# First FFN column pair by eight plain block products, with the token sums on VectorE and used from the second pair on

## The chip, the cores and the metric

The kernel runs on one core of a Trainium2 chip. A core has a matrix engine (TensorE, in the profile PE), three engines for elementwise work (VectorE or DVE, ScalarE or ACT, GpSimd or POOL), and a queue (SyncE or SP) that issues DMAs between the chip's memory and the core's on-chip buffers. Each engine takes its instructions in a fixed order and waits for others through semaphores. TensorE writes to eight banks of 128 x 512 float32 (PSUM), from which ScalarE and VectorE copy results out. The metric is the device time of one execution in microseconds (us).

## What is computed

The reference is one layer of a sequence encoder over 1024 tokens of width 1024: three token mixers (two kinds of attention and a state-space scan) merged through gates, then a gated MLP with a causal depthwise convolution. The change touches the MLP's first matrix product alone:

```python
def conv_ffn(h, w_up, conv_w, conv_b, w_down):
    a = causal_dwconv(h @ w_up, conv_w, conv_b)        # 3 taps, along the tokens
    gate, val = jnp.split(a, 2, axis=-1)               # 2 x 2816 columns
    return (jax.nn.silu(gate) * val) @ w_down

x = x + merged @ w_out[l]
x = x + conv_ffn(rms_norm(x, norm_ffn_g[l]), ...)
```

## The kernel before

**Stages.** The mixers take most of the time. Then follow, without a break on TensorE, the output product (`wo`, lines 1326 to 1391) with the second norm, the FFN's up products (lines 1394 to 1525) and its down products (`dn`, line 1628 the matmul). Every float32 product is made of three matmuls on a high and a low part of each operand: high x high, high x low, low x high. `split` (lines 142 and 143) makes the parts: ScalarE rounds to the high part, VectorE subtracts it to get the low part.

**Pairs.** The up product has 2 x 22 blocks of 128 columns. Pair i is gate block i and value block i + 22. A product (`product`, line 1321) is 12 matmuls: one 128-column block, four blocks of 128 input rows, 512 tokens, three part combinations. With the tokens in two halves and the input rows in two halves, the normed input is four blocks: B11 and B21 (first 512 tokens, input rows 0 to 511 and 512 to 1023), B12 and B22 (last 512 tokens). Computed directly, a pair is eight products, two for each of gate and value in each half of the tokens.

**Seven products.** The kernel uses a Strassen-Winograd scheme with seven products for each pair. On the side of the weights it needs S12 (two sums and differences of gate and value blocks) and S34 (two more), made by `sums` on GpSimd (lines 1411 to 1415) and then split into wh and wl; h22 is the split lower half of the value block. On the side of the tokens it needs T1 = B12 - B11, T3 = B22 - B12, T2 = T3 + B11 and T4 = B21 - T2. T1 takes the place of B12 in the norm itself (`norm2`); T3 is kept there in float32 as `T3f`. Once, at the first pair, `t_split` splits T3f into cbh and cbl (four blocks each, lines 1444 and 1447), `t_sums(True)` turns T3f into T2 in place (1454, 1455), which is split, and `t_sums(False)` turns it into T4 (1457, 1458), which is split. In `t_sums` blocks 0 and 1 are summed on VectorE, 2 and 3 on GpSimd. A pair's products are, by bank: `ua` gate x B11, then gate x B21 into the same bank; `ub` S12 x T2; `uc` S12 x T1, then S34 x B22; `ud` S34 x T3, then h22 x T4. A second product into a bank starts after ScalarE has copied out the first (to cg at 1431 or 1473, e5 at 1491, e7 at 1496). VectorE and GpSimd combine the copies to cg (gate) and cv (value), the convolution runs as ScalarE and VectorE steps (`fa`, 1517 and 1520), then SiLU (1523), a multiplication (1524) and a store to `act_d`.

**Early gate products.** Of the first four pairs (FIRST = 4) the two `ua` products, which need no T2, T3 or T4, are made ahead: B11 products of 0, 1 and 2, the last tile's norm, their B21 products, then both products of 3. So the loop has five products for each of pairs 0 to 3 and seven from pair 4 on.

**Order and buffers.** TensorE's order is that of the code; the other engines' order is set by a scheduler when the kernel is built. Raw weight blocks of a pair (tag wr) have two buffers, one for the gate and one for the value block; the gate block's is free when S34 has been made, the value block's when h22 has been split. S12, S34 and h22 have one buffer each; wh and wl have three in turn. Gate blocks 1 to 3 are loaded ahead into other buffers (tag t4).

## Time and profile before

| | us |
|---|---|
| median of 3 runs | 2163.03 |
| lowest and highest run | 2156.59, 2163.8 |
| the profiled execution | 2163.26 |
| its span in the profile | 2161.5 |

The profile covers one execution. Its views used below are the page's first lines (busy time of each engine), the chain of waits that ended last, busy time by stretch, and the timeline, whose rows are: start in us, duration in us, engine, line, operation, output<-inputs, and in brackets the idle time before the instruction with what ended it. DVE, ACT and POOL starts are some 0.1 us earlier than the end of the instruction before, so that the cost of one in a row of several is read between starts.

### The profile page before, as it was taken

To read this page: it belongs to the slowest core of one execution; us is meant where nothing else is said; L and a number is where in the kernel's file an instruction comes from. 1 tells how busy PE (TensorE), PEld (TensorE's weight loads), DVE (VectorE), ACT (ScalarE), POOL (GpSimd) and SP (SyncE) were. 2 spreads that over 40 slices of the span, in tenths; PEclk is the share of its full clock that TensorE was granted. 3 is DMA by queue.
4 is the path that set the end of the run, shared out by engine and by line. 5 is a ranking of instruction groups with operands and counts; after the bars stand their busy time and mean duration, and the time that the engine had idled before them with its cause. 6 is when DMAs were issued, how large, how long until landed. Compare 5 with 4: busy or idle time off the path is not lost.

```text
span 2161.5 us, 29107 instructions
## 1 busy us (share of the span) xinstructions
PE 2053.6 (95%) x10239; PEld 1693.8 (78%) x10253; DVE 1406.9 (65%) x2574; ACT 933.7 (43%) x1669; POOL 689.9 (32%) x636
## 2 busy tenths in 40 slices
PE   7999899999999999999999999999889999999999
PEld 6898787778888787787666788888668888887887
DVE  6687477356656566665888446557976777665655
ACT  5554222145555555554445313223444444544432
POOL 2454132212222222220222022002655454441855
PEclk9999999999999999999999999999899999999999
DMA  5167668554343544524343556342122222229765
GB/s 168 33 186 223 228 211 247 196 147 126 100 131 108 125 125 107 128 87 119 92 117 94 169 178 209 116 151 79 39 88 88 78 88 78 87 71 346 250 210 194
DMA packets 276649, 303.61 MB, mean 140 GB/s; under 512 B 19308, under 2 KB 209784, under 8 KB 276504
## 3 DMA queue, kind: packets, MB, share of 16 engines
q1 hardware_dynamic: 276504, 301.76, 45.5%
q8 instruction: 81, 1.33, 0.3%
q14 instruction: 64, 0.52, 0.1%
HBM read 209.03 MB, written 92.67 MB: 140 GB/s over the span
## 4 chain that ended last, share of the span: by engine, by line
PE 76%; DVE 10%; DMA 5%; ACT 3%; issue 3%; POOL 2%; SPq 0%; DVEq 0%; ACTq 0%; POOLq 0%
PE mm L794 15%; PE dn L1628 10%; PE ybr L167 8%; PE ua L1321 5%; PE uc L1321 4%; PE ud L1321 4%; PE wo L1366 4%; PE fx L167 4%; PE s L884 4%; PE tp L952 3%; PE ub L1321 2%; PE cq L167 1%; PE fxv L167 1%; PE q L167 1%; PE kv L167 1%
## 5 line engine op out<-in xcount | busy, mean ns | idle before, releaser
L794 PE MATMUL mm<-hnh,wh 128*128 128x512 f32 x576 | 251.5, 437 | 0.0
L906 POOL TENSOR_SCALAR pm<-pm,rs 128x128 f32<-128x128 f32 (+7 forms) x128 | 109.6, 859 | 407.3 <-DVE rs L905 256.2
L794 PE MATMUL mm<-hnh,wl 128*128 128x512 f32 x576 | 228.1, 396 | 0.0
L794 PE MATMUL mm<-hnl,wh 128*128 128x512 f32 x576 | 227.3, 395 | 0.0
L1628 PE MATMUL dn<-dr,dr 128*128 128x512 f32 x592 | 182.2, 389 | 0.0
L899 ACT ACTIVATE pm<-s,nmx 128x128 f32<-128x128 f32 (+2 forms) x192 | 110.0, 578 | 98.7 <-DVE nmx L896 69.8
L958 DVE TENSOR_TENSOR ptl<-tp,pth 128x512 fp32r<-128x512 f32 (+1 forms) x160 | 100.3, 633 | 69.7 <-ACT pth L957 68.0
L889 DVE TENSOR_REDUCE nmx<-s 128x1 f32<-128x128 f32 (+2 forms) x192 | 105.6, 553 | 58.8 <-PE s L887 47.0
L884 PE MATMUL s<-qk,qk 96*128 96x384 f32 (+5 forms) x480 | 122.3, 359 | 12.7 <-ACT pm L899 11.0
L957 ACT ACTIVATE pth<-tp 128x512 fp32r<-128x512 f32 (+1 forms) x160 | 88.0, 553 | 100.7 <-PE tp L952 100.2
L1628 PEld LDWEIGHTS dn<-dr,dr 128*128 128x128 f32 x592 | 111.1, 188 | 23.1
L794 PEld LDWEIGHTS mm<-hnh,wl 128*128 128x128 f32 x576 | 109.1, 189 | 25.6
L794 PEld LDWEIGHTS mm<-hnl,wh 128*128 128x128 f32 x576 | 110.2, 191 | 17.8 <-issue 3.4
L794 PEld LDWEIGHTS mm<-hnh,wh 128*128 128x128 f32 x576 | 110.7, 192 | 17.1 <-issue 3.3
L1628 PE MATMUL dn<-dr 128*128 128x512 f32 x296 | 115.2, 389 | 0.0
L167 PE MATMUL fx<-w5h,hnh 128*128 128x512 f32 x256 | 101.9, 403 | 7.0 <-ACT w5h L142 7.0
L143 DVE TENSOR_TENSOR dr<-dr,dr 128x1024 fp32r<-128x1024 f32 x52 | 73.0, 1403 | 54.3 <-ACT dr L142 52.4
L142 ACT ACTIVATE wh<-wr 128x1024 fp32r<-128x1024 f32 (+1 forms) x46 | 41.9, 911 | 144.5 <-PE ybr L167 63.5
L884 PEld LDWEIGHTS s<-qk,qk 96*128 96x128 f32 (+1 forms) x480 | 82.2, 194 | 25.6 <-ACT pm L899 15.0
L167 PE MATMUL fx<-w5h,hnl 128*128 128x512 f32 x256 | 101.8, 399 | 0.0
L167 PE MATMUL ybr<-ah,wh 128*128 128x512 f32 x256 | 99.6, 394 | 1.6 <-ACT ah L142 1.6
L167 PE MATMUL fx<-w5l,hnh 128*128 128x512 f32 x256 | 101.1, 396 | 0.0
(457 smaller groups left out, 5819.1 us busy)
## 6 DMA issues: line engine op xcount, KB each, us to landing
dr<-act_d SPq DMA_DIRECT2D x99, 256.0 KB
wr<-in_ffn_w_up_dram SPq DMA_DIRECT2D x47, 512.0 KB
wr<-in_w_in_dram SPq DMA_DIRECT2D x36, 512.0 KB
g_d<-t SPq DMA_DIRECT2D x24, 512.0 KB
gl<-g_d SPq DMA_DIRECT2D x24, 512.0 KB
ws<-in_ffn_w_down_dram SPq DMA_DIRECT2D x22, 512.0 KB
wsum_d<-ws SPq DMA_DIRECT2D x22, 512.0 KB
act_d<-fa SPq DMA_DIRECT2D x22, 512.0 KB
```

The lines of the kernel that those rows point to most:

```text
L143: return i, le.tensor_sub(l, src, f32(h))
L167: T.matmul(ps, a(k), b(k), start=(i == 0), stop=(i == n - 1))
L794: T.matmul(ps, a[:, k, :], b[half][:, k, :], start=(k == 0 and i == 0), stop=(k == NK - 1 and i == 2))
L884: T.matmul(ps[:, :w], q_[:, qs], k_[:, a:a + w], start=i_ == 0, stop=not last and i_ == len(o.passes) - 1)
L889: later(c + 0.1, lambda ps=ps, ci=ci, a=a, b=b: V.reduce_max(nmx[:, ci:ci + 1], ps[:, :b - a], axis=AX, negate=True))
L899: pss[ci][1][0] = later(c + 0.9 + 0.1 * ci, lambda ci=ci, a=a, b=b: A.activation(p_[:, a:b], pss[ci][0][:, :b - a], AF.Exp, bias=nb, accum ...
L906: G.tensor_scalar(p_[:, 0:n * P], p_[:, 0:n * P], rs[:, 3:4], 0.0, op0=ALU.mult, op1=ALU.add)
L957: later(c + 0.05, lambda th=th, pt=pt, off=off: A.activation(th[:, :off], pt[:, :off], AF.Copy))
L958: pl[0] = later(c + 0.6, lambda th=th, tl=tl, pt=pt, off=off: V.tensor_sub(tl[:, :off], pt[:, :off], f32(th[:, :off])))
L1321: T.matmul(ps, a, b, start=first and n == 0, stop=n == 11, skip_group_check=not first)
L1366: T.matmul(p, a, b, start=k == 0 and i == 0, stop=k == NK - 1 and i == 2)
L1628: T.matmul(ps[m], a[:, ts_], b[:, 512:], start=first_ and j == 0 and q == 0, stop=j == NFH - 1 and q == 2, skip_group_check=not first_)
```

## The change

Pair 0 is computed directly: its eight products are gate and value block against B11, B21, T1 and B22. With T1 in the place of B12, the products of the last 512 tokens get the first half's B11 product added, on VectorE (lines 1499 and 1500 of the changed kernel). S12, S34 and h22 aren't made for pair 0; the whole value block is split instead (hB). The early gate products go in the order 1, 2, 0 (`FORDER`), and those of block 3 follow pair 0's. All of `t_sums` is on VectorE. T3 is split at pair 0 as before, T2 after that; T4 is made and split within pair 1, where T2, T3 and T4 are used first. Pair 0's convolution (`finish_pair`) runs within pair 1.

```diff
@@ -1354,7 +1354,8 @@
     xrp = po_.enter_context(TP("x2p", 1))
     gff = bcast(norm_ffn_g[0], D, "gff", xrp)
     x2r = [None] * NT
-    first = []
+    first = {}
+    FORDER = (1, 2, 0, 3)
     units = [(t, nh) for nh in range(2) for t in range(3)] + [(t, nh) for t in range(3, NT) for nh in range(2)]
 
     head = [psp.tile([P, 512], F32, name=uid("wo"), tag="up", bufs=6) for _ in range(3)]
@@ -1370,14 +1371,14 @@
     for t, nh in units:
         ns = slice(512 * nh, 512 * nh + 512)
         if nh == 0 and 4 <= t < 4 + FIRST:
-            n = t - 4
+            n = FORDER[t - 4]
             if n == 0:
                 r0 = raws(pairs[0])
                 raw = r0[0]
             else:
                 raw = fpl.tile([P, NK, P], F32, name=uid("wr"), tag="t4", bufs=4)
                 SY.dma_start(raw, upv[:, :, pairs[n] * P:pairs[n] * P + P])
-            first.append(halves(raw) if n < 3 else raw)
+            first[n] = halves(raw) if n < 3 else raw
         if nh == 0:
             x2r[t] = xrp.tile([P, D], F32, name=uid("x2"), tag="x2", bufs=4)
             SY.dma_start(x2r[t], x[0, t * P:(t + 1) * P, :])
@@ -1396,10 +1397,14 @@
 
     B11, B21 = [(rows(h2h[0], k), rows(h2l[0], k)) for k in (0, 4)]
     T1, B22 = [(rows(h2h[1], k), rows(h2l[1], k)) for k in (0, 4)]
-    a_ = []
-    for n in range(3):
-        a_.append(bank("ua"))
+    a_, done_ = {}, {}
+
+    def p1(n):
+        a_[n] = bank("ua")
         product(a_[n], first[n], 0, *B11)
+
+    for n in FORDER[:3]:
+        p1(n)
     norm2(NT - 1, x2r[NT - 1])
     po_.close()
 
@@ -1415,22 +1420,20 @@
         G.tensor_sub(S34[:, 4:8, :], ri[:, 4:8, :], S12[:, 4:8, :])
         return S12, S34
 
-    S_ = sums(*r0)
-    h22_ = halves(r0[1][:, 4:8, :], 4)
-    done_ = []
-    for n in range(3):
-        c_ = upb.tile([P, S], F32, name=uid("cg"), tag="cg", bufs=FIRST)
-        A.activation(c_[:, 512:], a_[n], AF.Copy)
-        done_.append(c_)
-    for n in range(FIRST):
-        if n == 3:
-            first[n] = halves(first[n])
-            a_.append(bank("ua"))
-            product(a_[n], first[n], 0, *B11)
-            done_.append(upb.tile([P, S], F32, name=uid("cg"), tag="cg", bufs=FIRST))
-            A.activation(done_[n][:, 512:], a_[n], AF.Copy)
+    def keep_p1(n):
+        done_[n] = upb.tile([P, S], F32, name=uid("cg"), tag="cg", bufs=FIRST)
+        A.activation(done_[n][:, 512:], a_[n], AF.Copy)
+
+    def p2(n):
         product(a_[n], first[n], 4, *B21, first=False)
         A.activation(done_[n][:, 0:512], a_[n], AF.Copy)
+
+    for n in FORDER[:3]:
+        keep_p1(n)
+    p2(1)
+    hB = halves(r0[1])
+    p2(2)
+    p2(0)
     cbp = pcb.enter_context(TP("cb", 1))
     cbh = cbp.tile([P, 12, 512], F32R, name="cbh", tag="cbh")
     cbl = cbp.tile([P, 12, 512], F32R, name="cbl", tag="cbl")
@@ -1449,20 +1452,57 @@
     def t_sums(second):
 
         for k in range(4):
-            e = G if k > 1 else V
             if second:
-                e.tensor_add(tf[k], tf[k], f32(B11[0][k]))
-                e.tensor_add(tf[k], tf[k], f32(B11[1][k]))
+                V.tensor_add(tf[k], tf[k], f32(B11[0][k]))
+                V.tensor_add(tf[k], tf[k], f32(B11[1][k]))
             else:
-                e.tensor_sub(tf[k], f32(B21[0][k]), tf[k])
-                e.tensor_add(tf[k], tf[k], f32(B21[1][k]))
+                V.tensor_sub(tf[k], f32(B21[0][k]), tf[k])
+                V.tensor_add(tf[k], tf[k], f32(B21[1][k]))
 
     def tmp(name, bufs=1):
         return upa.tile([P, 512], F32, name=uid(name), tag=name, bufs=bufs)
 
-    for n, i in enumerate(pairs):
+    def finish_pair(i, cg, cv):
+        av = []
+        for j, c in ((i, cg), (i + NFF, cv)):
+            a = fpl.tile([P, S], F32, name=uid("fa"), tag="t4", bufs=4)
+            A.activation(a, c, AF.Identity, bias=pc_f2[:, 44 + j:45 + j], scale=pc_f2[:, j:j + 1])
+            for d in (1, 2):
+                w = pc_f1[:, 44 * (2 - d) + j:44 * (2 - d) + j + 1]
+                V.scalar_tensor_tensor(out=a[:, d:], in0=c[:, :S - d], scalar=w, in1=a[:, d:],
+                                       op0=ALU.mult, op1=ALU.add)
+            av.append(a)
+        A.activation(av[0], av[0], AF.Silu)
+        V.tensor_mul(av[1], av[0], av[1])
+        SY.dma_start(act_d[i], av[1])
+
+    t_split(T3)
+    b0 = bank("ub")
+    product(b0, hB, 0, *B11)
+    f1 = tmp("e5")
+    A.activation(f1, b0, AF.Copy)
+    product(b0, hB, 4, *B21, first=False)
+    cv = fpl.tile([P, S], F32, name=uid("cv"), tag="t4", bufs=4)
+    A.activation(cv[:, 0:512], b0, AF.Copy)
+    t_sums(True)
+    c0_ = bank("uc")
+    product(c0_, first[0], 0, *T1)
+    product(c0_, first[0], 4, *B22, first=False)
+    t_split(T2)
+    first[3] = halves(first[3])
+    d0 = bank("ud")
+    product(d0, hB, 0, *T1)
+    product(d0, hB, 4, *B22, first=False)
+    p1(3)
+    keep_p1(3)
+    p2(3)
+    V.tensor_add(done_[0][:, 512:], c0_, done_[0][:, 512:])
+    V.tensor_add(cv[:, 512:], d0, f1)
+    plain = (pairs[0], done_[0], cv)
+
+    for n, i in list(enumerate(pairs))[1:]:
         early = n < FIRST
-        ri, rj = r0 if n == 0 else raws(i)
+        ri, rj = raws(i)
         if early:
             cg = done_[n]
         else:
@@ -1472,11 +1512,14 @@
             product(a0, hA, 0, *B11)
             A.activation(cg[:, 512:], a0, AF.Copy)
         e1 = cg[:, 512:]
-        S12, S34 = S_ if n == 0 else sums(ri, rj)
+        S12, S34 = sums(ri, rj)
         hS12 = halves(S12)
         hS34 = halves(S34)
-        h22 = h22_ if n == 0 else halves(rj[:, 4:8, :], 4)
-        if n > 0:
+        h22 = halves(rj[:, 4:8, :], 4)
+        if n == 1:
+            t_sums(False)
+            t_split(T4)
+        else:
             b0 = bank("ub")
             product(b0, hS12, 4, *T2)
         if not early:
@@ -1484,20 +1527,14 @@
         c0_ = bank("uc")
         product(c0_, hS12, 0, *T1)
         d0 = bank("ud")
-        if n == 0:
-            t_split(T3)
         product(d0, hS34, 0, *T3)
         e5 = tmp("e5")
         A.activation(e5, c0_, AF.Copy)
-        if n == 0:
-            t_sums(True)
-            t_split(T2)
         e7 = tmp("e7")
         A.activation(e7, d0, AF.Copy)
         product(c0_, hS34, 4, *B22, first=False)
-        if n == 0:
-            t_sums(False)
-            t_split(T4)
+        if n == 1:
+            finish_pair(*plain)
             b0 = bank("ub")
             product(b0, hS12, 4, *T2)
         X = tmp("X", 2)
@@ -1511,20 +1548,7 @@
         G.tensor_add(cv[:, 512:], X, Y)
         V.tensor_add(cg[:, 512:], c0_, X)
         V.tensor_add(cv[:, 0:512], d0, X)
-        av = []
-        for j, c in ((i, cg), (i + NFF, cv)):
-            a = fpl.tile([P, S], F32, name=uid("fa"), tag="t4", bufs=4)
-            A.activation(a, c, AF.Identity, bias=pc_f2[:, 44 + j:45 + j], scale=pc_f2[:, j:j + 1])
-            for d in (1, 2):
-                w = pc_f1[:, 44 * (2 - d) + j:44 * (2 - d) + j + 1]
-                V.scalar_tensor_tensor(out=a[:, d:], in0=c[:, :S - d], scalar=w, in1=a[:, d:],
-                                       op0=ALU.mult, op1=ALU.add)
-            av.append(a)
-        A.activation(av[0], av[0], AF.Silu)
-        V.tensor_mul(av[1], av[0], av[1])
-        SY.dma_start(act_d[i], av[1])
-
-
+        finish_pair(i, cg, cv)
 
 
     wd = ffn_w_down[0].rearrange("(r p) c -> r p c", p=P)
```

Three places show how the instructions now stand. First GpSimd, from the last tile's norm on. S_4621 and S_4622 are S12 and S34 of pair 0, S_4648 and S_4649 those of pair 1; before:

```order
L1411 TENSOR_TENSOR S_4621_15530<-wr_15047 128x512
L1414 TENSOR_TENSOR S_4622_15533<-wr_15045,wr_15047 128x512
L1412 TENSOR_TENSOR S_4621_15530<-S_4621_15530,wr_15045 128x512
L1415 TENSOR_TENSOR S_4622_15533<-wr_15045,S_4621_15530 128x512
L1411 TENSOR_TENSOR S_4648_15763<-wr_15761 128x512
L1412 TENSOR_TENSOR S_4648_15763<-S_4648_15763,wr_15759 128x512
L1454 TENSOR_TENSOR T3f<-T3f,hnh_13413 128x512 x2
L1455 TENSOR_TENSOR T3f<-T3f,hnl_13415 128x512 x2
L1414 TENSOR_TENSOR S_4649_15766<-wr_15759,wr_15761 128x512
L1415 TENSOR_TENSOR S_4649_15766<-wr_15759,S_4648_15763 128x512
L1510 TENSOR_TENSOR Y_15743<-e_4638_15667,e_4639_15685 128x512
L1457 TENSOR_TENSOR T3f<-hnh_13413,T3f 128x512 x2
```

Now, S_4637 and S_4638 being those of pair 1, S_4659 and S_4660 those of pair 2:

```order
L1416 TENSOR_TENSOR S_4637_15728<-wr_15726 128x512
L1419 TENSOR_TENSOR S_4638_15731<-wr_15724,wr_15726 128x512
L1417 TENSOR_TENSOR S_4637_15728<-S_4637_15728,wr_15724 128x512
L1420 TENSOR_TENSOR S_4638_15731<-wr_15724,S_4637_15728 128x512
L1416 TENSOR_TENSOR S_4659_15863<-wr_15861 128x512
L1417 TENSOR_TENSOR S_4659_15863<-S_4659_15863,wr_15859 128x512
L1419 TENSOR_TENSOR S_4660_15866<-wr_15859,wr_15861 128x512
L1420 TENSOR_TENSOR S_4660_15866<-wr_15859,S_4659_15863 128x512
L1547 TENSOR_TENSOR Y_15843<-e_4647_15788,e_4648_15790 128x512
L1548 TENSOR_TENSOR cv_15842<-X_15828,Y_15843 128x512
```

Pair 0's four sums and the eight token sums (T3f) are gone, so that the sums of pairs 1 and 2 follow each other.

Second, ScalarE around the splits of T2 and T4 (cbh, the second and third group of four). cg_15602 and ua_15589 are gate block 3, cg_15544 is gate block 2, e_4638 and e_4639 are e5 and e7 of pair 0, wh_15769 is S12 of pair 1; before:

```order
L1433 ACTIVATE cg_15542<-ua_15455 128x512
L1444 ACTIVATE cbh<-T3f 128x512 x4
L142 ACTIVATE wh_15629<-S_4622_15533 128x1024
L1433 ACTIVATE cg_15544<-ua_15468 128x512
L1431 ACTIVATE cg_15602<-ua_15589 128x512
L142 ACTIVATE wh_15769<-S_4648_15763 128x1024
L1433 ACTIVATE cg_15602<-ua_15589 128x512
L1491 ACTIVATE e_4638_15667<-uc_15633 128x512
L1444 ACTIVATE cbh<-T3f 128x512 x4
L1496 ACTIVATE e_4639_15685<-ud_15646 128x512
L1444 ACTIVATE cbh<-T3f 128x512 x2
```

Now, with cg_15707 and ua_15694 for gate block 3, cg_15534 for block 0, cv_15622 for pair 0's value, wh_15734 and wh_15738 for S12 and S34 of pair 1, wh_15869 for S12 of pair 2:

```order
L1483 ACTIVATE e_4627_15608<-ub_15595 128x512
L1486 ACTIVATE cv_15622<-ub_15595 128x512
L1447 ACTIVATE cbh<-T3f 128x512 x4
L142 ACTIVATE wh_15734<-S_4637_15728 128x1024
L1447 ACTIVATE cbh<-T3f 128x512 x2
L1469 ACTIVATE fa_15804<-cg_15534,pc_f_122 128x1024
L1447 ACTIVATE cbh<-T3f 128x512
L142 ACTIVATE wh_15738<-S_4638_15731 128x1024
L1447 ACTIVATE cbh<-T3f 128x512
L1425 ACTIVATE cg_15707<-ua_15694 128x512
L1469 ACTIVATE fa_15808<-cv_15622,pc_f_122 128x1024
L142 ACTIVATE wh_15869<-S_4659_15863 128x1024
```

The copies of gate block 3 stood ahead of T2's split; the first of them now stands behind the last block of T4's.

Third, SP's queue from the last residual store (x_d) on. wr_15759 and wr_15761 are gate and value block of pair 1, the two after them those of pair 2; before:

```order
L1389 DMA x_d<-x_4575_15250 128x1024
L1304 DMA wr_15759<-in_ffn_w_up_dram 128x8x128
L1304 DMA wr_15761<-in_ffn_w_up_dram 128x8x128
L1389 DMA x_d<-x_4591_15347 128x1024
L1304 DMA wr_15867<-in_ffn_w_up_dram 128x8x128
L1304 DMA wr_15869<-in_ffn_w_up_dram 128x8x128
L1525 DMA act_d<-fa_15752 128x1024
L1304 DMA wr_15975<-in_ffn_w_up_dram 128x8x128
```

Now wr_15726 is the value block of pair 1, wr_15859 and wr_15861 are pair 2, wr_15967 and wr_15969 pair 3:

```order
L1390 DMA x_d<-x_4575_15250 128x1024
L1390 DMA x_d<-x_4591_15347 128x1024
L1304 DMA wr_15726<-in_ffn_w_up_dram 128x8x128
L1304 DMA wr_15859<-in_ffn_w_up_dram 128x8x128
L1304 DMA wr_15861<-in_ffn_w_up_dram 128x8x128
L1304 DMA wr_15967<-in_ffn_w_up_dram 128x8x128
L1477 DMA act_d<-fa_15808 128x1024
L1304 DMA wr_15969<-in_ffn_w_up_dram 128x8x128
L1477 DMA act_d<-fa_15852 128x1024
L1304 DMA wr_16075<-in_ffn_w_up_dram 128x8x128
```

Pair 1's gate block (wr_15724) is no longer here: it now stands right behind pair 0's two blocks, ahead of the residual's stores. The store of pair 0's result now stands between the two loads of pair 3.

## Prediction

> **What bounds the kernel now.** I read the first lines of the page, then the chain of work that ended last, and then cut the span at the places the chain names.
>
> ```profile
> span 2161.5 us, 29107 instructions
> PE 2053.6 (95%) x10239; PEld 1693.8 (78%) x10253; DVE 1406.9 (65%) x2574; ACT 933.7 (43%) x1669; POOL 689.9 (32%) x636
> ...
> 1616.97 2.72 PE ud L1321 x12
> 1619.69 2.72 PE ua L1321 x12
> ```
>
> The first two lines say that TensorE (PE) is the bound nearly everywhere. The last two are from the chain: one product of the FFN stage is 12 matmuls and takes 2.72 us, and from 1619.69 on, where pair 5 begins, the chain is TensorE alone. So the change is worth what it does before that point. The same stage by phase (columns: length, then busy time and count of each engine, then the granted clock):
>
> ```profile
> core 0: us, PE busy (x) PEld busy (x) DVE busy (x) ACT busy (x) POOL busy (x), PEclk, DMA share, GB/s
> 1494.86:1561.62 66.76, 58.36 (x228) 43.70 (x227) 57.00 (x61) 30.25 (x45) 34.23 (x20) 0.87 0.16 50
> 1512.59:1541.23 28.64, 23.03 (x82) 15.64 (x80) 28.61 (x24) 11.09 (x18) 23.40 (x14) 0.84 0.06 18
> 1561.62:1619.69 58.07, 49.38 (x205) 39.04 (x205) 42.90 (x37) 25.47 (x30) 33.59 (x20) 0.97 0.28 89
> 1619.69:1941.00 321.31, 321.31 (x1417) 265.30 (x1416) 224.42 (x202) 156.02 (x185) 155.86 (x98) 1.00 0.25 82
> ```
>
> After 1619.69 TensorE never idles. Before it there are two lossy phases. From 1494.86 to the end of pair 1 stand 18 products (eight gate products of pairs 0 to 3, five of pair 0, five of pair 1), 18 x 2.72 = 49.0 us of work in 66.6. From there to pair 5 stand 17 products (5 + 5 + 7), 46.2 us in 58.1. What TensorE waited for in both:
>
> ```profile
> PE ud L1321 <- DVE cbl L1447: 4.0, 3, 2.0
> PE uc L1321 <- ACT e L1491: 4.0, 2, 2.8
> PE ua L1321 <- ACT cg L1473: 2.9, 1, 2.9
> PE ub L1321 <- DVE cbl L1447: 2.9, 3, 1.3
> ```
>
> Rows one and four, 6.9 us, are phase one: pair 0 waits for the low parts of T2 and T4, with VectorE (DVE) busy for 28.61 of 28.64 us. Rows two and three are phase two, and follow from a loop that feeds the pairs:
>
> ```profile
> 1529.23 19.19 SPq L1304 DMA_DIRECT2D wr<-in_ffn_w_up_dram  x2
> ...
> 1547.34 0.68 DVE L143 TENSOR_TENSOR l<-wr,h 128x512 fp32r<-128x512 f32 x1
> 1552.18 1.64 POOL L1411 TENSOR_TENSOR S<-wr 128x512 f32<-128x512 f32 x1 [10.24 <-DMA wr<-in_ffn_w_up_dram]
> 1565.73 0.68 DVE L143 TENSOR_TENSOR l<-wr,h 128x512 fp32r<-128x512 f32 x1
> 1582.89 0.69 DVE L143 TENSOR_TENSOR l<-wr,h 128x512 fp32r<-128x512 f32 x1
> 1601.81 0.68 DVE L143 TENSOR_TENSOR l<-wr,h 128x512 fp32r<-128x512 f32 x1
> ```
>
> The row l of pair n frees the value buffer, so that pair n+1's value block can be loaded, summed by GpSimd (POOL), split, and used. It repeats after 17.2 and 18.9 us, and l itself waits for the single h22 buffer, which the last product of the pair before releases. Pairs 1 to 3 give TensorE only 5 products, 13.6 us, so there the loop is the bound; from pair 5 on 7 products, 19.0 us, cover it. The loop's place is set by the end of pair 1.
>
> **The change part by part.**
>
> ```profile
> 1516.61 0.50 PE L1321 MATMUL ua<-hnh,wh 128*128 128x512 f32 x1 [0.69 <-ACT cg L1431]
> 1561.46 0.39 PE L1321 MATMUL ub<-cbh,wh 128*128 128x512 f32 x1
> 1588.55 0.50 PE L1321 MATMUL uc<-hnh,wh 128*128 128x512 f32 x1 [2.79 <-ACT e L1491]
> 1602.60 0.50 PE L1321 MATMUL ua<-hnh,wh 128*128 128x512 f32 x1 [2.88 <-ACT cg L1473]
> 1606.73 0.63 PE L1321 MATMUL uc<-hnh,wh 128*128 128x512 f32 x1
> 1613.92 0.50 PE L1321 MATMUL uc<-hnh,wh 128*128 128x512 f32 x1 [1.24 <-ACT e L1491]
> 1619.53 0.39 PE L1321 MATMUL ua<-hnh,wh 128*128 128x512 f32 x1
> ```
>
> *One product more.* Pair 0 needs 8 products in place of 7: +2.72 us of TensorE work, 19 in phase one. None of the eight needs T2, T3 or T4.
>
> *Start of phase one.* Seven products and the transposes come first in both kernels, then a second product into the same bank behind a ScalarE (ACT) copy: the row at 1516.61 stands, for pair 0's value bank now. Its weights, hB, are split where the first split of this stretch stands now:
>
> ```profile
> 1508.66 1.23 DVE L143 TENSOR_TENSOR wl<-wr,wh 128x1024 fp32r<-128x1024 f32 x1 [0.20 <-ACT wh L142]
> 1511.44 1.23 DVE L143 TENSOR_TENSOR wl<-S,wh 128x1024 fp32r<-128x1024 f32 x1 [0.95 <-ACT wh L142]
> 1512.59 2.39 DVE L1447 TENSOR_TENSOR cbl<-T3f,cbh 128x512 fp32r<-128x512 f32 x2
> ```
>
> That split ends at 1509.9, in time. Then run six products (that second one, two of pair 0's gate, two of its value, the first of block 3): 1516.61 + 0.13 for the restart + 6 x 2.72 = 1533.1.
>
> *The new wait.* Block 3's second product waits for the ScalarE copy of its first. In ScalarE's order that copy now stands behind the high part of T4's last block, which waits for the last sum on VectorE; behind the copy wait pair 0's value activation and pair 2's S12 split. So the sums must be timed. What a VectorE instruction costs with and without GpSimd beside it:
>
> ```profile
> 1516.60 0.68 DVE L1447 TENSOR_TENSOR cbl<-T3f,cbh 128x512 fp32r<-128x512 f32 x1
> 1517.20 0.68 DVE L1454 TENSOR_TENSOR T3f<-T3f,hnh 128x512 f32<-128x512 f32 x1
> 1517.81 1.77 DVE L1447 TENSOR_TENSOR cbl<-T3f,cbh 128x512 fp32r<-128x512 f32 x1
> 1519.50 0.68 DVE L1455 TENSOR_TENSOR T3f<-T3f,hnl 128x512 f32<-128x512 f32 x1
> ...
> 1517.36 1.68 POOL L1454 TENSOR_TENSOR T3f<-T3f,hnh 128x512 f32<-128x512 f32 x1 [1.23 <-DVE cbl L1447]
> 1540.67 1.27 POOL L1511 TENSOR_TENSOR cv<-X,Y 128x512 f32<-128x512 f32 x1 [1.23 <-DVE X L1504]
> ```
>
> By starts, a 512-wide instruction takes 0.61 us, and 1.69 when one of GpSimd stands beside it: +1.1. In the 28.64 us stretch above lie 22 VectorE instructions (its row counts two more that its edges cut), 20 of 0.61 and two wide splits of 1.15, or 14.5 us; the other 14.1 over the 13 GpSimd instructions wholly inside are again 1.1 each. So eight token sums taken off GpSimd save 8 x 1.1 = 8.8 us of VectorE's time, and cost it 8 x 0.61 = 4.9.
>
> Along the new VectorE order, from 1512.59 to the last sum of T4 stand 27 instructions of 512 (splits, 16 sums, pair 1's l, pair 0's gate addition) and one wide split: 27 x 0.61 + 1.15 = 17.6. Beside them fall five GpSimd instructions: pair 1's four S sums, which start near 1514 when its value block has landed (loaded after 1509.9, and from 1548.0, the end of l, to 1552.18 that took 4.1), and one of pair 2: 5.5. The last sum ends at 1512.6 + 17.6 + 5.5 = 1535.7, the copy 1.1 later (two ScalarE instructions): TensorE resumes at 1536.8, **3.7 us of new wait**. Bounds: nothing above the copy's own 0.7 if GpSimd fell elsewhere, 5.9 with two GpSimd instructions more.
>
> The Trainium skill, "SBUF — State Buffer", section "Who interferes with whom", says that a VectorE instruction with two SBUF inputs and a GpSimd one that reads SBUF exclude each other for the whole instruction. The trace agrees in kind, but by it the lockout would be GpSimd's own 1.27 us, an estimate of 6.4 in place of 5.5.
>
> *End of phase one.*
>
> ```profile
> 1543.55 1.27 DVE L1520 SCALAR_TENSOR_TENSOR fa<-cg,pc_f,fa 128x1023 f32<-128x1023 f32 x1
> 1548.25 1.06 ACT L1523 ACTIVATE fa<-fa 128x1024 f32<-128x1024 f32 x1
> 1601.97 0.57 ACT L1473 ACTIVATE cg<-ua 128x512 f32<-128x512 f32 x1
> ```
>
> Block 3's second product and pair 1's five make 6 x 2.72 = 16.3, with 0.3 of restart. Before its fourth product pair 1 waits for the ScalarE copy e5, which stands behind pair 0's SiLU, and that behind the second convolution step on VectorE: after the last sum two such steps (1.2 by starts, the first row), four of 0.61 and one split, with two GpSimd hits, end at 1535.7 + 8.2 = 1543.9; SiLU (second row) and the copy (as the third) end at 1545.5. TensorE is there at 1536.8 + 0.15 + 3 x 2.72 = 1545.1: 0.4 of wait. After the 2.88 us wait at 1602.60 a product took 4.13 us, after the 2.79 us wait at 1588.55 none did; I take 0.7 between nothing and 1.4. Sum: 1536.8 + 17.7 = 1554.5, against 1561.46: **7.0 earlier**, one product more included.
>
> The Trainium skill, "TensorE: Matmul & The Clock Gate", section "HAM oscillation — how this bites in real kernels", warns of idle gaps above some 3.4 us, after which the array runs at half rate. By it the new wait would cost an estimated 1.7 (one such window at half rate) in place of 0.7. The trace agrees in part: the 4.13 us came after 2.88 us of idle, less than that limit.
>
> *Phase two.* Pair 2's value block no longer waits for T4: its buffer is free once pair 1's h22 is split, and that h22 is the first user of its buffer. So pair 2's products follow at once, and the loop starts from pair 2's l, behind the end of pair 1. On VectorE an addition (0.61), a convolution step (1.2) and l itself (0.61) stand in between, with one GpSimd hit: 3.5 (now 1566.41 - 1561.46 = 4.95). So l ends at 1558.0, 8.4 earlier. The loop's two laps to the restart at 1602.60 keep their length, 1602.60 - 1566.41 = 36.2: 1594.2. From there to pair 5 took 16.9; the 1.24 wait at 1613.92 goes, since e5 now stands ahead of the S12 split in ScalarE's order: 15.7, pair 5 at 1609.9 in place of 1619.53. **Gain 9.6 us.** The order behind is the same but for a few loads and one split of the down stage, and TensorE is full, so it carries to the end.
>
> *Edits at no cost.* The first blocks' new order, 1, 2, 0, and pair 0's four S sums gone: both lie beside wo products before 1494.86, where TensorE is full; without that cover the sums' 8 x 1.1 us on VectorE would show. On SP's queue pair 1's gate load now stands ahead of the residual's stores and waits for pair 0's gate split:
>
> ```profile
> 1417.66 1.23 DVE L143 TENSOR_TENSOR wl<-wr,wh 128x1024 fp32r<-128x1024 f32 x1 [1.76 <-ACT wh L142]
> 1424.08 0.34 SPq L1389 DMA_DIRECT2D x_d<-x  x1
> ```
>
> The split ends before the store behind it can go, so nothing is late. The convolution of pair 0 moves into pair 1, beside its products; its cost on VectorE is in the walk.
>
> **Sum.** The profiled execution took 2163.26 us, 1.76 outside its span and 0.2 above the median of 2163.03. 2163.26 - 9.6 = **2153.7 us**.
>
> **The rivals.**
>
> *A: the loop eats it.* If both laps take 18.9 and 19.0 (-1.75), l follows after 4.95 (-1.45), the clock costs 1.3 (-0.6) and the 1.24 stays, the gain is 4.6; with two GpSimd hits more, 2.4: 2158.7 to 2160.9. For: the loop's length hangs on loads and sums that the change leaves. Against: l has less ahead of it.
>
> *B: TensorE becomes the bound.* If the loop hides, pair 5 starts 17 x 2.72 = 46.2 after 1554.5, at 1600.7: gain 18.8, 2144.4; without the new wait 2140. For: the e5 copy moves ahead of SiLU in pair 3. Against: pair 4's load waits for l of pair 3, 17 us after the one before, and TensorE needs 13.6.
>
> *C: VectorE alone isn't quicker.* If its slow instructions are not GpSimd's doing, all keep the stretch's mean, 28.6/22 = 1.30 us; then the last sum comes at 1512.6 + 27 x 1.30 + 1.15 = 1548.9, 13.2 later than I have it, and the copy of block 3 holds TensorE there. Loop and pair 5 shift with it: 13.2 - 9.6 = 3.6 us **slower** than before, 2166.9. It decides from 1.17 us an instruction on. Against: 0.68 and 1.77 alternate in step with GpSimd's rows.
>
> **How the numbers follow.** The forecast, 2148 to 2156.5, gets 0.60; A 0.18; B 0.15; C 0.07. 0.3% is 6.5 us, about what a measurement can tell from none: faster (under 2156.5) is forecast and B, 0.75; same is A, 0.18; slower 0.07. The range reaches from B's price with the wait to A's middle, **2144 to 2160**.
>
> **What would show it.** Right: no wait of a T2, T3 or T4 product for cbl; one wait of 2 to 6 us of ua on cg (the copy of block 3) near 1533; pair 1's products end near 1554, pair 2's l near 1558, pair 5 starts near 1610; VectorE's sums at 0.68 while GpSimd is idle. Wrong: sums at 1.3 or more with GpSimd idle, the waits of phase two gone (B) or grown by what phase one saved (A), or a TensorE wait after pair 5.

## The result and the profile after

| | before | changed |
|---|---|---|
| median, us | 2161.82 (4 runs) | 2146.89 (4 runs) |
| lowest to highest | 2156.59 to 2163.8 | 2146.41 to 2151.41 |
| profiled execution | 2163.26 | 2146.99 |
| its span | 2161.5 | 2145.2 |

The ratio is 0.9938 with a 95% interval of 0.9922 to 0.9953: faster by 0.62%. The medians lie 14.9 us apart, where 9.6 were forecast.

The page's first lines for the changed kernel:

```profile
span 2145.2 us, 29128 instructions
PE 2047.2 (95%) x10265; PEld 1693.2 (79%) x10265; DVE 1398.4 (65%) x2579; ACT 934.2 (44%) x1667; POOL 670.0 (31%) x622
```

From its chain of waits (start, length, what) the two products behind a wait (length with the modelled end), and the end of the FFN's start:

```profile
1533.25 4.60 PE ua L1321 x12
...
1589.16 4.40 PE ua L1321 x12
...
1618.68 3.02 PE uc L1321 x12
1621.70 2.72 PE ud L1321 x12
```

From 1618.68, the sixth product of pair 5, the chain is TensorE alone up to the down stage; before it was so from the first product of pair 5. That pair now starts at 1604.29, forecast near 1610, before at 1619.53. What TensorE waited for from the first FFN product to the end, the five largest (columns: sum in us, times, longest):

```profile
PE ua L1321 <- ACT cg L1425: 2.6, 1, 2.6
PE ua L1321 <- ACT cg L1513: 2.5, 1, 2.5
PE dn L1652 <- DVE wl L143: 1.7, 1, 1.7
PE ub L1321 <- ACT e L1483: 0.7, 1, 0.7
PE uc L1321 <- ACT e L1532: 0.6, 1, 0.6
```

The waits for cbl, 6.9 us before, are gone. The first row is the new wait, at block 3's second product. The stages, by busy time in windows (length, then each engine's busy time and count, then the granted clock); the borders are the first FFN product, the first product of pair 2, pair 5's first, and the start of the long run of `dn`. The first three rows are the changed kernel's:

```profile
1493.13:1551.53 58.40, 55.10 (x239) 44.62 (x238) 50.91 (x66) 30.14 (x44) 19.41 (x10) 0.97 0.17 55
1551.53:1604.29 52.76, 49.14 (x206) 38.95 (x205) 41.45 (x37) 24.76 (x30) 31.17 (x18) 0.97 0.28 90
1604.29:1937.32 333.03, 330.58 (x1454) 272.16 (x1453) 235.04 (x210) 161.48 (x190) 157.80 (x99) 1.00 0.26 85
```

and these are the same three of the kernel before, with the same borders:

```profile
1494.86:1561.46 66.60, 58.20 (x228) 43.55 (x226) 56.84 (x61) 30.09 (x45) 34.07 (x20) 0.87 0.15 49
1561.46:1619.53 58.07, 49.38 (x205) 39.05 (x204) 42.90 (x37) 25.47 (x30) 33.75 (x20) 0.97 0.28 89
1619.53:1951.65 332.12, 330.31 (x1455) 272.22 (x1453) 233.28 (x210) 160.74 (x189) 156.74 (x98) 1.00 0.26 85
```

The two spans differ by 16.3 us. Of these 8.2 are phase one, 5.3 phase two, minus 0.9 the stage behind; 1.7 lie ahead of the first FFN product and 2.0 in `dn`, where little was changed. The first experiments ask whether those two count.

### The profile page after: what moved, and what is told of

The parts are those of the page before. It is cut to its first block, busy times and chain, and to the rows that moved or that the text cites. A ratio compares the mean times of both kernels' runs of the same rounds, so it can differ in the third digit from the quotient of the medians.

```text
span 2145.2 us, 29128 instructions
## 1 busy us (share of the span) xinstructions
PE 2047.2 (95%) x10265; PEld 1693.2 (79%) x10265; DVE 1398.4 (65%) x2579; ACT 934.2 (44%) x1667; POOL 670.0 (31%) x622
## 4 chain that ended last, share of the span: by engine, by line
PE 76%; DVE 9%; DMA 5%; POOL 3%; ACT 3%; issue 3%; SPq 1%; ACTq 0%; DVEq 0%; POOLq 0%
PE mm L794 15%; PE dn L1652 10%; PE ybr L167 8%; PE ua L1321 5%; PE uc L1321 5%; PE ud L1321 4%; PE wo L1367 4%; PE fx L167 4%; PE s L884 4%; PE tp L952 3%; PE ub L1321 2%; PE fxv L167 1%; PE kv L167 1%; PE q L167 1%; DMA raw<-in_w_in_dram 1%
## 5 line engine op out<-in xcount | busy, mean ns | idle before, releaser
L143 DVE TENSOR_TENSOR dr<-dr,dr 128x1024 fp32r<-128x1024 f32 x52 | 72.0, 1385 | 52.9 <-ACT dr L142 49.3
L884 PEld LDWEIGHTS s<-qk,qk 96*128 96x128 f32 (+1 forms) x480 | 82.7, 195 | 26.1 <-ACT pm L899 15.4
```

Of the source, the lines that this page charges most:

```text
L143: return i, le.tensor_sub(l, src, f32(h))
L884: T.matmul(ps[:, :w], q_[:, qs], k_[:, a:a + w], start=i_ == 0, stop=not last and i_ == len(o.passes) - 1)
```

## The experiments

Lengths in the tables are, for each profile, phase one, phase two and their sum (first FFN product to pair 5), between the same borders as above.

**r1, r9, r10: the two kernels again, unchanged.**

> The changed kernel once more, untouched, beside the kernel before: how far the two profiled spans can be taken at their word. In the first pair of profiles the changed kernel stood 1.73 us ahead already at the first product of the FFN (1493.13 against 1494.86 us), where both run the same instructions in the same order, and gained 1.5 us more inside the last stage, whose products are the same. Theory: these 3.2 us are scatter of single executions, and the change is worth what lies between, 13.0 us or so: median 2148 to 2149. Rival: they belong to the change (the new order of the first four weight blocks reaches back into the stage ahead): the first product starts at 1493.1 us again to within 0.3 us, and the median is 2146 to 2147.

> The kernel before once more, for a second profile of it. Theory: its way from the first FFN product to pair 5 is fixed by the queues and stays 124.7 us within 1 us, as the changed kernel's did (111.2, 112.0, and 112.0 in r5), while the time ahead of the first product moves by 2 to 5 us from execution to execution. Rival: the 124.67 us of the first profile were a long one, and what the change gains there is smaller: 122 us or less.

> The changed kernel again, to stand beside the next two on one chip: 13 to 16 us under the kernel before; 111 to 112 us from the first FFN product to pair 5.

| profile | first FFN product at | phase one | phase two | sum | pair 5 to `dn` | `dn` to the end |
|---|---|---|---|---|---|---|
| before | 1494.86 | 66.60 | 58.07 | 124.67 | 332.12 | 209.85 |
| r9, before | 1491.73 | 65.92 | 57.24 | 123.16 | 332.21 | 209.90 |
| changed | 1493.13 | 58.40 | 52.76 | 111.16 | 333.03 | 207.88 |
| r1, changed | 1490.34 | 58.40 | 53.55 | 111.95 | 332.84 | 209.47 |
| r10, changed | 1492.33 | 58.42 | 53.50 | 111.92 | 332.67 | 209.48 |

r1 took 2143.48 us against 2157.86 for the kernel before on the same chip (0.9936, interval 0.9923 to 0.995), r10 2147.57 against 2159.07 (0.9944, 0.9927 to 0.9962). Between executions of one kernel the time ahead of the first product moves by 3 us, and `dn` of the changed kernel by 1.6. So both differences lie within scatter, as the theory of r1 had it. (The short `dn`, 207.9 us, comes back in r4, r7, r11 and r12; whether the kernel before ever has it, two profiles can't tell.) Of the expected numbers, r1's median of 2148 to 2149 was missed, but the kernel before was lower beside it too (2157.86 for 2161.82). r10 gained 11.5 us where 13 to 16 were expected, and r9's 123.16 us to pair 5 lie between its theory (124.7 within 1) and its rival (122 or less).

To pair 5 one kernel's executions agree within 1.5 us. By the means the change is worth 7.9 us in phase one and 4.4 in phase two, and gives 0.7 back behind: **11.6 us**. The three medians show 14.9, 14.4 and 11.5, on average 13.6, so that another 2 us ahead of the first product or in `dn` are not excluded.

**r2 and r3: one half of the change at a time.** r2 is the kernel before with

```diff
-            e = G if k > 1 else V
+            e = V
```

> The kernel before with the sixteen token sums all on VectorE, pair 0 as it was. Theory (both halves of the change count, the sums less): GpSimd's eight token sums go; each cost the VectorE instruction beside it 1.1 us (1.77 against 0.68), 8.8 us in all, and VectorE takes eight more at 0.60 by starts, 4.8 us, so the last split of T4 and the value split behind it come 4.0 us earlier and the loads and sums of the pairs behind follow: 2157.8, range 2156 to 2160. Rival 1, the sums alone are the change: 2147. Rival 2, the plain products alone are it, and the sums only have to be somewhere: 2161.8, within 1 us of the kernel before.

r3 is the changed kernel with `e = G if k > 1 else V` back in `t_sums`, its operations on `e`.

> The changed kernel with the token sums of blocks 2 and 3 given back to GpSimd, pair 0 still by eight plain products. Theory: eight more GpSimd instructions beside VectorE take 8.8 us from it and give back 4.8, so the last T4 sum comes 4.0 us later; it stands ahead of the copy that block 3's second product waits for, and TensorE has no other work there, so the wait goes from 2.6 to 6.6 us: 2151, range 2148 to 2153. Rival 1, the sums alone are the change: 2161.8. Rival 2, the plain products alone: 2147, within 1 us of the changed kernel. A third possibility, that GpSimd is so much slower that VectorE waits for it: above 2154.

| | time, us | ratio to before, interval | phase one | phase two | sum |
|---|---|---|---|---|---|
| r2, sums only | 2151.18 | 0.9969, 0.9958 to 0.9979 | 62.22 | 55.58 | 117.80 |
| r3, plain products only | 2157.55 | 0.9999, 0.9986 to 1.0011 | 70.21 | 52.78 | 122.99 |

(The kernel before took 2157.86 beside both.) Phase one of r2 is 4.0 us shorter than the mean of before, the 4.0 expected; phase two added 2.1 that were not, and in time r2 gained 6.7 us, more than its range (some 2 to 6). The working behind the 4.0 was not quite right either: T4's last split ends 5.7 us earlier, and not 4.0 (44.9 after the first product for 50.6). GpSimd not only lost its token sums; its next sum for pair 1 no longer slowed VectorE either. It was held up itself, while VectorE ran one instruction behind the other, the 512-wide ones at 0.6 each:

```profile
1515.80 13.63 POOL L1414 TENSOR_TENSOR S<-wr,wr 128x512 f32<-128x512 f32 x1 [4.18 <-DVE wl L143]
```

r3 missed by far: with the sums divided, the plain products gain nothing in time. It lies where its third possibility had it (above 2154), but not for that reason, VectorE waiting for GpSimd. Its own profile says where the gain is lost. In order of time, TensorE's wait, and ScalarE's queue around the copy it waits for:

```profile
1547.28 0.79 PE L1321 MATMUL ua<-hnh,wh 128*128 128x512 f32 x1 [13.97 <-ACT cg L1425]
...
1536.99 0.63 ACT L1447 ACTIVATE cbh<-T3f 128x512 fp32r<-128x512 f32 x1 [0.60 <-POOL T3f L1461]
1537.53 1.04 ACT L142 ACTIVATE wh<-S 128x1024 fp32r<-128x1024 f32 x1
1544.39 1.28 ACT L1476 ACT_TABLE_LOAD   x1 [5.82 <-DVE fa L1473]
1545.68 1.06 ACT L1476 ACTIVATE fa<-fa 128x1024 f32<-128x1024 f32 x1
1546.64 0.58 ACT L1425 ACTIVATE cg<-ua 128x512 f32<-128x512 f32 x1
```

The wait is 14.0 us, not 6.6. T4's last upper half ends 41.8 us after the first FFN product, 2.2 later than in the changed kernel (39.6) and not the 4.0 expected; but the scheduler, which sets ScalarE's order, has also put pair 0's SiLU ahead of the copy, and that waits for VectorE's convolution. So r3 mixes two things, and r7 below takes them apart.

**r4 and r11: the copy first.** The copy of block 3 is issued ahead of T4's last two upper halves and of pair 1's second split:

```diff
-        A.activation(done_[n][:, 512:], a_[n], AF.Copy)
+        return A.activation(done_[n][:, 512:], a_[n], AF.Copy)
...
-    keep_p1(3)
+    kept = keep_p1(3).ins
...
-        hS34 = halves(S34)
+        with tc.issue_after(kept) if n == 1 else ExitStack():
+            hS34 = halves(S34)
...
-            i = A.activation(t[0][k], tf[k], AF.Copy)
+            with tc.issue_after(kept) if t is T4 and k > 1 else ExitStack():
+                i = A.activation(t[0][k], tf[k], AF.Copy)
```

> The changed kernel with block 3's first copy queued on ScalarE ahead of T4's last two upper halves and of pair 1's second split, so that it no longer stands behind the token sums. Theory: the copy starts at its product's end, about 1530.9 instead of 1532.63 us, the wait of block 3's second product falls from 2.6 to about 0.8 us, the product behind it takes 2.8 instead of 4.45 us since TensorE is no longer idle that long, and all behind it follows: 3.4 us less than the changed kernel, 2143.5. Rival 1: what stands idle is made up by the next wait, since pair 4's value block and its sums come from a chain that does not start at TensorE: 2146.9. Rival 2: the product behind the wait is slow for another reason than the idle time: 1.8 us less, 2145.1.

> r4 again, on one chip with r10. Theory: the 2.5 to 3.3 us by which its way to pair 5 was shorter than the changed kernel's are real, and show as 1 to 3 us under r10 in the median. Rival: they are given back in the stages behind, or lie under the scatter: within 1 us of r10.

The changed kernel's waits in this stretch are in the first two rows (from r1), r4's largest in the last two:

```profile
1530.46 0.50 PE L1321 MATMUL ua<-hnh,wh 128*128 128x512 f32 x1 [2.61 <-ACT cg L1425]
1540.45 0.50 PE L1321 MATMUL uc<-hnh,wh 128*128 128x512 f32 x1 [1.51 <-ACT e L1532]
```

```profile
1532.62 0.50 PE L1321 MATMUL ua<-hnh,wh 128*128 128x512 f32 x1 [0.69 <-ACT cg L1425]
1542.57 0.50 PE L1321 MATMUL uc<-hnh,wh 128*128 128x512 f32 x1 [0.65 <-ACT e L1534]
```

The wait fell from 2.6 to 0.7, as expected, and phase one from 58.4 to 56.5, 1.9 us. The expected 3.4 counted a slow product that cost nothing: in the first profile of the changed kernel the product behind the wait took 4.45 us (1533.25 to 1537.70), in r1 and r10 2.88, and phase one is 58.4 in all three. Where the product is quick, pair 1 waits 1.5 us longer for the copy e5, which stands behind pair 0's SiLU. To pair 5 r4 took 108.66 us and r11 109.66, some 2.5 less than the changed kernel. The medians don't settle it. r4 took 2143.86 (0.9938, 0.9923 to 0.9952), near its expected 2143.5, but the changed kernel beside it (r1) took 2143.48, so that this hit was luck. r11 took 2143.42 (0.9932, 0.9915 to 0.9948), 4.2 less than r10 beside it and more than the 1 to 3 of its theory, with overlapping runs (2138.78 to 2147.72 and 2139.49 to 2151.82).

**r7: sums divided again, but the copy first.** r3 with the edit of r4, and pair 0's convolution behind the copy as well:

```diff
-            finish_pair(*plain)
+            with tc.issue_after(kept):
+                finish_pair(*plain)
```

> The changed kernel with the token sums of blocks 2 and 3 given back to GpSimd, as in r3, but with block 3's first copy queued ahead of what stood before it there (T4's last two upper halves, pair 1's second split, and pair 0's scaling, table load and SiLU). In r3 the copy stood 14.0 us behind its product. Theory A (the place of the sums counts only through that queue): the wait falls to 1 us or less, VectorE's splits of pair 1's S12 and S34 come 1 to 2 us late for TensorE in its place, and from the first FFN product to pair 5 it takes 109 to 112 us, where r3 took 123.0, the changed kernel 111.2 and 112.0, r4 108.7: 12 to 15 us under the kernel before. Rival B (the sums on VectorE carry the gain themselves, since VectorE beside GpSimd is late for everything behind): the wait moves to pair 1's splits, 118 to 123 us, 0 to 6 us under the kernel before.

```profile
1524.07 0.50 PE L1321 MATMUL ua<-hnh,wh 128*128 128x512 f32 x1 [0.69 <-ACT cg L1425]
1528.23 0.50 PE L1321 MATMUL uc<-hnh,wl 128*128 128x512 f32 x1 [0.70 <-DVE wl L143]
1534.29 0.50 PE L1321 MATMUL uc<-hnh,wh 128*128 128x512 f32 x1 [0.61 <-ACT e L1535]
1542.00 0.50 PE L1321 MATMUL ud<-cbh,h 128*128 128x512 f32 x1 [1.98 <-ACT e L1537]
```

Theory A, in the wait and in the lengths: 59.03 and 52.87, 111.90 us to pair 5, and 2143.72 us against 2160.71 (0.9938, 0.9918 to 0.9958). (By the medians that is 17.0 us, where 12 to 15 were expected, and the late splits cost TensorE 0.7, not 1 to 2.) The 14.0 us wait is 0.7, and with the sums half on GpSimd the plain products now gain what the whole change gains. So the 11 us to pair 5 by which r3 was longer were a matter of ScalarE's order. Against r4 and r11, r7 is 2.2 to 3.2 us longer. These differ from it in the place of the sums and in that of pair 0's convolution in ScalarE's queue, and no run parts the two.

To pair 5, against a mean of 123.9 us before, the gains are: sums alone 6.1, plain products alone 0.9, or 12.0 with the copy first; both 12.2, or 14.8 with the copy first. They don't add up; both halves act on the same waits for T2 and T4.

**r5, r6 and r8: a second buffer for h22.** The first edit is r5, the control; r6 has it and the second, which doubles `h22` and `l22`; r8 is r6 with the edit of r4:

```diff
-        X = tmp("X", 2)
+        X = T3f[:, n % 2, :]
...
-        Y = tmp("Y")
+        Y = T3f[:, 2, :]
```

```diff
-            h, l = (upb.tile([P, n, P], F32R, name=uid(t), tag=t) for t in ("h22", "l22"))
+            h, l = (upb.tile([P, n, P], F32R, name=uid(t), tag=t, bufs=2) for t in ("h22", "l22"))
```

> The changed kernel with its temporaries X and Y laid into the store of the raw token sums T3f, which nothing uses once T4 is split (it frees 6 KB a partition for the next two runs and is their control). Every theory: as the changed kernel, 14.4 us under the kernel before, within 1.5 us; pair 4's second product waits 2.5 us as before. A dependence on T4's split that held the first X back would show as a new wait of TensorE in pair 1.

> As r5, with two buffers for the split of a pair's fourth quarter, h22 and l22. Theory: what is left of the FFN's start (the 2.5 us wait of pair 4's second product, the 0.5 and 0.5 us of its first splits, and up to 1.5 us of a slow product behind the wait) hangs on one buffer: the value block's last reader, the split into l22, waits for TensorE to be through the pair before it, and only then does the block's buffer take the next load. With a second buffer the split and the load run one pair ahead, and these 3.5 to 5 us go: 18 to 19.5 us under the kernel before. Rival: another single buffer binds just behind it (S12 and S34, which the next pair's sums overwrite, or the four buffers of split weights), and the waits stay or move: within 1.5 us of r5.

> r4 and r6 in one: block 3's first copy ahead in ScalarE's queue, and two buffers for h22 and l22. r4 shortened the way from the first FFN product to pair 5 by 2.5 to 3.3 us against the two profiles of the changed kernel, yet its median was no lower. Theory: what r4 gained is real and was drowned in the 2 to 3 us by which single executions differ ahead of the FFN; with the loop's wait gone as well it adds to r6's gain: 20 to 22 us under the kernel before, and 104 to 106 us from the first FFN product to pair 5. Rival: both shorten the same chain: as r6, within 1 us.

r5 took 2148.0 us against 2160.71 (0.9949, 0.9932 to 0.9965), 112.04 us to pair 5, as the changed kernel. That is 12.7 us gained, a little under the 14.4 within 1.5 that were expected; its stage behind pair 5 is 2.5 us longer, with a wait of 3.0 at the start of `dn`. r6 took 2165.65 (1.003, 1.0017 to 1.0043) and r8 2168.83 (1.0045, 1.0028 to 1.0062): both slower than the kernel before, against every theory. The 2.5 us wait did go, but in r6 pairs 2 and 3 wait 1.2 and 3.2 us for e5 (nothing and 0.5 in r5), and it needs 111.70 to pair 5, r8 113.14. The loss is behind it. From pair 5 to `dn`, the window of r6, its largest wait of TensorE, and the window of r5:

```profile
1601.80:1955.22 353.42, 334.59 (x1455) 271.33 (x1453) 286.31 (x210) 159.92 (x189) 186.82 (x99) 1.00 0.26 81
```

```profile
PE ua L1321 <- ACT cg L1513: 14.6, 15, 1.9
```

```profile
1601.76:1937.11 335.35, 331.31 (x1455) 272.26 (x1453) 233.46 (x211) 161.20 (x190) 157.04 (x98) 1.00 0.27 87
```

With as many instructions (one less, one more by the borders) VectorE is busy for 53 us more, GpSimd for 30 more. The 72 convolution steps account for VectorE's share; a quarter of them, in r5 and then in r6 (columns: busy us, mean ns, and idle time before):

```profile
L1472 DVE SCALAR_TENSOR_TENSOR fa<-cg,pc_f,fa 128x1023 f32<-128x1023 f32 x18 | 23.0, 1278 | 1.4 <-ACT fa L1469 1.4
L1472 DVE SCALAR_TENSOR_TENSOR fa<-cg,pc_f,fa 128x1023 f32<-128x1023 f32 x18 | 39.5, 2195 | 1.4 <-ACT fa L1469 1.4
```

One pair of r6, GpSimd and then ScalarE, shows how that reaches TensorE:

```profile
1640.24 1.30 POOL L1416 TENSOR_TENSOR S<-wr 128x512 f32<-128x512 f32 x1 [9.58 <-DMA wr<-in_ffn_w_up_dram]
1641.50 2.27 POOL L1547 TENSOR_TENSOR T3f<-e,e 128x512 f32<-128x512 f32 x1
1643.73 2.27 POOL L1417 TENSOR_TENSOR S<-S,wr 128x512 f32<-128x512 f32 x1
1645.97 1.73 POOL L1548 TENSOR_TENSOR cv<-T3f 128x512 f32<-128x512 f32 x1
...
1647.73 1.24 ACT L1469 ACTIVATE fa<-cv,pc_f 128x1024 f32<-128x1024 f32 x1 [4.85 <-POOL cv L1548]
1648.88 0.58 ACT L1513 ACTIVATE cg<-ua 128x512 f32<-128x512 f32 x1
```

The loads come earlier, so GpSimd makes the sums (S) a pair further ahead than in r5, where a pair's Y (the row with T3f<-e,e) and cv come after the sums for the next pair are done. In r6 one sum for the pair after next stands ahead of Y and waits for its load, and another stands between Y and cv, all of it beside VectorE's convolution. So the scaling that reads cv is late, and the copy that TensorE waits for stands behind it, some 1 us in 15 of the pairs.

**r12: the second copy of that kind.** r4, with pair 3's convolution issued behind pair 4's first copy:

```diff
-            A.activation(cg[:, 512:], a0, AF.Copy)
+            kept = A.activation(cg[:, 512:], a0, AF.Copy).ins
+            if n == FIRST:
+                with tc.issue_after(kept):
+                    finish_pair(*late)
...
-        finish_pair(i, cg, cv)
+        if n == FIRST - 1:
+            late = (i, cg, cv)
+        else:
+            finish_pair(i, cg, cv)
```

> r4 with the second wait of that kind taken away too: pair 3's scaling and SiLU are issued behind pair 4's first copy, which in the changed kernel's profile stood 6.3 us behind its product (1582.28 to 1588.54 us), behind a scaling that waited for GpSimd's sum. Theory: the wait of pair 4's second product, 2.5 us in every profile so far, goes, and with it the slow product behind it where there is one: 105.5 to 107 us from the first FFN product to pair 5, and 2 to 4 us under r10 in the median. Rival: pair 4's second split, ready about 1588.4 us, is the next bound, and the products wait there instead: 108 us, as r11.

```profile
1583.09 0.50 PE L1321 MATMUL ua<-hnh,wh 128*128 128x512 f32 x1 [0.66 <-ACT cg L1514]
1595.69 0.50 PE L1321 MATMUL uc<-hnh,wh 128*128 128x512 f32 x1 [4.16 <-ACT e L1537]
...
1594.09 1.06 ACT L142 ACTIVATE wh<-S 128x1024 fp32r<-128x1024 f32 x1 [4.47 <-POOL S L1417]
1595.06 0.58 ACT L1537 ACTIVATE e<-uc 128x512 f32<-128x512 f32 x1
```

The 2.5 us went, and 4.2 came three products later: pair 4's e5 copy now stands behind a split for pair 5 that waits for GpSimd. Phase two is 56.24 instead of 52.1 and 53.2, and the median 2146.39 (0.9945, 0.9931 to 0.9958) is 1.2 us under r10's, where 2 to 4 were expected. The rival was right that something binds next, and wrong in what.

No run is shown to beat the changed kernel. r4's edit has the shortest way to pair 5 in both of its profiles, and medians 0.4 us above and 4.2 below the changed kernel's; that it is better by some 2 us is likely, not shown.

## Why the prediction was right, and its sizes too small

The mechanism was the one forecast: the waits for T2 and T4 went, one new wait came where it was put, pair 2's loop started earlier, and the wait of the loop stayed. The sizes were mostly too small. Its steps in order; the trace's numbers are counted from the first FFN product, since the start moves from run to run.

*Start of phase one: 0.9 us more than charged.* The restart at 1516.61 (21.75 after the start) stood, but came at 20.90. The transposes of the last tile had waited in the kernel before, and no longer do, the rows of before and then of the changed kernel:

```profile
1503.94 0.74 PE L1281 MATMUL pt<-ident,xn 128*128 128x128 f32 x5 [0.65 <-ACT cg L1423]
```

```profile
1501.41 1.03 PE L1281 MATMUL pt<-ident,xn 128*128 128x128 f32 x8
```

*The new wait: right in kind, 2.6 us for 3.7.* It stood where the prediction put it, behind T4's last upper half (ScalarE's rows):

```profile
1532.11 0.61 ACT L1447 ACTIVATE cbh<-T3f 128x512 fp32r<-128x512 f32 x1
1532.63 0.58 ACT L1425 ACTIVATE cg<-ua 128x512 f32<-128x512 f32 x1
```

VectorE's walk, forecast at 23.1 us, took 21.8 (1509.95 to 1531.79), with four GpSimd instructions slowing it and not five. The fifth began in time, but gave way: it took 3.40 us itself, the sums beside it kept their 0.6, and only the convolution step behind the walk was slow:

```profile
1513.46 1.76 DVE L1456 TENSOR_TENSOR T3f<-T3f,hnh 128x512 f32<-128x512 f32 x1
1518.54 0.68 DVE L1457 TENSOR_TENSOR T3f<-T3f,hnl 128x512 f32<-128x512 f32 x1
1531.11 0.68 DVE L1460 TENSOR_TENSOR T3f<-T3f,hnl 128x512 f32<-128x512 f32 x1
...
1511.27 1.72 POOL L1416 TENSOR_TENSOR S<-wr 128x512 f32<-128x512 f32 x1 [23.80 <-DMA wr<-in_ffn_w_up_dram]
1516.44 1.62 POOL L1420 TENSOR_TENSOR S<-wr,S 128x512 f32<-128x512 f32 x1
1530.12 3.40 POOL L1416 TENSOR_TENSOR S<-wr 128x512 f32<-128x512 f32 x1 [12.05 <-DVE wl L143]
```

The price of 0.6 alone and 1.7 beside GpSimd held to the row; rival C, VectorE no quicker alone, is refuted.

*End of phase one: 7.0 forecast, 8.2 against the profile it was made from, 7.9 by the means.* Behind the wait 1.1 us were charged for a slow product (0.7) and for e5 (0.4). They came as one or the other, never both, about 1.6 us in each of the three profiles: the copy e5 has its own time behind SiLU, and TensorE is early for it unless it is slow. The copy in the first profile, with the slow product, and in r1, without:

```profile
1542.60 0.58 ACT L1532 ACTIVATE e<-uc 128x512 f32<-128x512 f32 x1
```

```profile
1539.82 0.58 ACT L1532 ACTIVATE e<-uc 128x512 f32<-128x512 f32 x1
```

Counted from the first FFN product both start at 49.5.

*Phase two: 2.6 forecast, 4.4 measured (means).* This is the step that was sized worst. From pair 2's first product to the end of its l: 3.5 forecast, 3.07 in all three profiles (4.95 before). From there to the restart of pair 4's second product: 36.2 "keep their length"; it took 34.6, 35.2 and 35.1 (36.2 and 35.4 before). From the restart to pair 5: 15.7 forecast, 15.1 to 15.4 (16.9 before). Each part erred to the same side, and the 36.2 was a long one of two. The l of the changed kernel is this row, which ends 3.07 us behind the start of pair 2's first product at 1551.53:

```profile
1553.92 0.68 DVE L143 TENSOR_TENSOR l<-wr,h 128x512 fp32r<-128x512 f32 x1
```

r3 and r7, with the sums divided, have the phase two of the changed kernel, 52.8 and 52.9, and the same short way to l (3.1). r2, with the sums alone, still needs 4.9 to l, but 15.4 from the restart to pair 5. So the early l comes with the plain products, and the 1.5 us behind the restart come with either half. Which of the instructions beside the loop moved, wasn't tried.

*Behind pair 5: nothing forecast, 0.7 lost.* A wait of 0.6 us at pair 5's second uc product, for e5 behind a split that waits for GpSimd, is in all three profiles of the changed kernel and in none of before. "It carries to the end" held but for that; a TensorE wait after pair 5 was among the signs of being wrong, and this is a small one.

*The sum.* 11.6 us of effect for 9.6; 11.6 lies in the interval of every median (the first one's, 0.9922 to 0.9953, is 10 to 17 us), and the rest of 14.9 lies in what the table shows to move from run to run. That rest took the median, 2146.89, 1.1 us below the band of 2148 to 2156.5 that the forecast was given 0.60 for, into the part of the range that stood for B. By the stage lengths the change belongs in the band (2163.0 - 11.6 = 2151.4). Of the rivals, A (the loop eats it) erred in direction: phase two gave more than forecast, not less. B (the loop hides, 18.8) did not happen: the wait at pair 4's second product, 2.5 us, stayed. What the prediction did not see is how much hung on the queue: it priced the copy behind T4's sums, and by r3 the plain products are worth nothing where the sums stay divided and SiLU comes to stand ahead of that copy.

## What to carry to other kernels

A copy that frees a TensorE bank for its next product belongs at the head of its engine's queue; what a scheduler put ahead of it decided more here than on which engine the sums were made (14.0 us of wait in r3, 0.7 in r7, with the sums on the same engines). When a wait is taken away, look for the next instruction of the same queue that the waiting engine needs: in r12 and r6 it took back more than was won. Measure a stage from its own first instruction when the run around it moves by more than the effect.

## What the runs showed of the hardware that was not expected

After an idle gap TensorE sometimes runs the next product slowly and sometimes doesn't, for the same gap: after 2.62, 2.61 and 2.62 us at the same product of the same kernel the next took 4.45, 2.88 and 2.88 us; after 2.55 us at pair 4's second product 2.85 in r4 and 4.14 in r11. Of the 17 gaps of 2.5 to 3.0 us in the up products of the fourteen profiles, 11 were followed by a product of 4.1 us or more and 6 by one of 2.9 or less. So a slow product can't be charged to a gap of this size, only allowed for. The Trainium skill, "TensorE: Matmul & The Clock Gate", section "HAM oscillation — how this bites in real kernels", names gaps above some 3.4 us; these were shorter.

A second engine's earlier start can cost more than its waiting: in r6 the same VectorE and GpSimd instructions took 53 and 30 us more of busy time in the up stage, once GpSimd's sums fell beside VectorE's convolution.

The price of running beside each other does not always fall on VectorE. In the changed kernel four GpSimd instructions of 1.6 to 1.7 us each took 1.1 us from VectorE, while in r2 one GpSimd instruction, 1.27 us when alone, took 13.63 and VectorE, with two-input instructions one right behind the other, lost nothing. What decides between the two was not tried.
